# Strassen sums of the right sides: from sums of rows that are then transposed, to sums of transposed blocks

## The chip, the cores and the metric

The kernel runs on one core of a Trainium2 chip. The metric is the device time of one execution in microseconds (us), and the time of a kernel is the median of several executions. The engines are named as the profile names them: PE (TensorE: matmuls and transposes), DVE (VectorE), ACT (ScalarE), POOL (GpSimd) and SP (SyncE, which issues most DMAs).

## The reference, cut to what matters

The reference is one layer of a causal decoder in float32: 1024 positions, width 1024. Two feed-forward blocks (FFNs) of the same form enclose a mixing stage (sparse attention and stick-breaking attention, side by side):

```python
x = x + 0.5 * swiglu(rms_norm(x, g_ffn1), w1_gate, w1_up, w1_down)
...
x = x + 0.5 * swiglu(rms_norm(x, g_ffn2), w2_gate, w2_up, w2_down)

def swiglu(h, w_gate, w_up, w_down):
    return (jax.nn.silu(h @ w_gate) * (h @ w_up)) @ w_down
```

The change touches `h @ w_gate` and `h @ w_up` of both FFNs (w: 1024 x 2816), and of these only how the right sides of the products are made from h.

## The kernel before

**Numbers.** Every matmul of a product is made of three: each operand is split into a high part rounded to the matmul's type (`fp32r`) and a low part, the rest. `halve` makes both: ACT writes the high part into the left half of a tile (L377), DVE or POOL writes source minus high part into its right half (L378). A product is then high x high, high x low and low x high (L468 to L470 in `times`).

**Blocks.** The products are computed transposed, weights on the left and h transposed on the right. h is cut into four blocks of 512 x 512: B11 and B21 are the left and right column halves of the first 512 rows, turned, B12 and B22 those of the last 512. The class `Right` holds them as four tiles of 128 x 1024 (high and low) per block. For the first pair of weight column blocks (p = 0) the products are plain, eight half products, in `opening`; from p = 1 on they follow Strassen's scheme in `products`, with seven products per weight matrix, whose right sides are B11, B21, B22 and the sums T1 = B12 - B11, T2 = B22 - T1, T3 = B22 - B12 and T4 = B21 - T2. So the opening has a second task: to have T1 to T4 ready for the loop.

**How the sums are made before the change.** `Right.sum` subtracts rows that aren't turned (four DVE instructions of 128 x 512 per sum, L435), and `Right.turn` turns the result: 16 transposes on PE (128 x 128 each, L427) into four PSUM banks (`pst`), from which `halve` makes high and low part.

**PSUM.** There are eight banks, two for each letter a, b, c, d. A bank that is asked for again under a letter waits until all that read the one before the last are done. B12 and B22 are turned with letters c and d, T1 to T3 with a and b, c and d being in use for products.

**What sets the order.** In `ffn_in`, the first iteration stands in a manual schedule: PE, DVE, ACT and POOL take their instructions in the order written in `opening`. The loop behind it is ordered by the framework's scheduler. Each engine works its queue in order, and waits at an instruction whose inputs or buffers aren't ready. Transfers are issued by SP, with the loads of weights held back by free buffers and, in the first FFN, the splitting of `w_in` beside the loop paced by matmuls (`beside`).

**Around it.** In the first FFN B11 and B21 are turned at the start, from rows normed right before; in the second, between the two halves of the output projection of the mixing stage (`between`). In both, B12 and B22 are turned in the middle of the opening, once the last rows are normed (L414).

**Names.** In the trace `aB`, `aT`, `ay` belong to the first FFN, `bB`, `bT`, `by` to the second: blocks, sums, rows of B11 and B21. `a00A`, `a10A` are the opening's left sides of gate and up weights, `a01A` and `a01S` those of the loop's first products, `a01s` the sums for them (L457 to L460), `asg` the activated gate and its product with the other side (L522, L525), `as` the sums of the results for the next stage (L589 to L592), `a0u` the accumulated products (L481 to L491).

## Time and profile before

| | us |
|---|---|
| median of three runs | 2219.55 |
| lowest and highest of them | 2217.72, 2219.59 |
| the profiled execution, its own time | 2216.6 |
| its span, first to last instruction | 2214.8 |

| engine | busy us | share of the span | instructions |
|---|---|---|---|
| PE | 2156.8 | 97% | 10460 |
| DVE | 1524.3 | 69% | 2548 |
| ACT | 1103.8 | 50% | 2169 |
| POOL | 858.1 | 39% | 698 |

The first FFN's opening lies from 21 to 82 us, its loop to about 457; the second's opening from about 1562 to 1622. Matmuls are pipelined: a row gives each its own length (0.39 us) although one starts every 0.23, so what a group of them costs is read from starts. A row of the timeline gives start, length, engine, line, what is written and read, count, and in brackets how long the engine had been idle and what released it.

### The profile page before, as it was taken

How to read it: one execution, taken by the hardware profiler on the slowest of the kernel's cores; microseconds unless marked ns; L12 is line 12 of the kernel's file. 1: busy time of each engine (PE TensorE's matmuls, PEld its weight loads, DVE VectorE, ACT ScalarE, POOL GpSimd, SP SyncE). 2: the span in 40 equal slices, each digit the busy share in tenths (PEclk: the TensorE clock that was granted, in tenths of full speed). 3: DMA queues.
4: the chain of work that ended last, by engine and by line, in shares of the span. 5: the costliest groups of instructions: out<-in, count | busy, mean ns of one | idle time of the engine just before them, and what ended most of it. 6: DMA issues, size and time to landing. Idle time of an engine off the chain costs nothing.

```text
span 2214.8 us, 30577 instructions
## 1 busy us (share of the span) xinstructions
PE 2156.8 (97%) x10460; PEld 1800.9 (81%) x10460; DVE 1524.3 (69%) x2548; ACT 1103.8 (50%) x2169; POOL 858.1 (39%) x698
## 2 busy tenths in 40 slices
PE   7999999999999999899999899999999999999999
PEld 6888888888879888688788688878888888888877
DVE  5575767688874598677787687754565555678685
ACT  5333333335454358999987565533333232233443
POOL 3355555523245445211111322264255554552233
PEclk9999999999999999999999999999999999999999
DMA  5487878497675343665654522565133232359655
GB/s 172 94 252 204 243 215 232 169 318 248 213 196 165 112 143 110 202 178 156 168 166 161 199 91 94 204 226 198 63 99 106 94 109 95 113 171 326 225 167 186
DMA packets 269052, 381.01 MB, mean 172 GB/s; under 512 B 23264, under 2 KB 157040, under 8 KB 268896
## 3 DMA queue, kind: packets, MB, share of 16 engines
q1 hardware_dynamic: 256384, 339.17, 49.7%
q0 software_dynamic: 12512, 39.89, 4.9%
q8 instruction: 82, 1.34, 0.3%
q14 instruction: 74, 0.61, 0.1%
HBM read 259.94 MB, written 119.05 MB: 171 GB/s over the span
## 4 chain that ended last, share of the span: by engine, by line
PE 80%; ACT 7%; DVE 6%; DMA 3%; issue 2%; POOL 1%; SPq 0%; ACTq 0%; DVEq 0%; POOLq 0%
PE p L681 6%; PE p L682 6%; PE p L680 5%; PE pc L468 4%; PE pd L468 4%; PE pd L469 4%; PE pd L470 4%; PE pc L469 4%; PE pc L470 4%; PE pa L468 3%; PE pa L469 3%; PE pa L470 3%; ACT junka L1194 3%; PE psf L308 2%; PE psf L309 2%
## 5 line engine op out<-in xcount | busy, mean ns | idle before, releaser
L1194 ACT ACTIVATE junka<-u,cand,sig 128x768 bf16<-128x768 f32 (+4 forms) x186 | 183.7, 988 | 5.6 <-DVE cand L1191 4.0
L1635 DVE TENSOR_TENSOR_SCAN left<-left 128x640 f32<-128x640 f32 (+3 forms) x64 | 86.3, 1349 | 4.0 <-ACT left L1627 4.0
L802 ACT ACTIVATE swh<-swr 128x512 fp32r<-128x512 f32 x48 | 30.2, 628 | 117.2 <-issue 47.8
L1128 POOL DMA_DIRECT2D gd<-evg x32 | 17.9, 561 | 152.6 <-ACT evg L1125 112.8
L803 DVE TENSOR_TENSOR swr<-swr,swh 128x512 f32<-128x512 f32 x48 | 41.1, 856 | 43.0 <-ACT swh L802 42.9
L1684 DVE TENSOR_TENSOR pt<-pstT,pt 128x512 fp32r<-128x512 f32 (+1 forms) x96 | 50.8, 550 | 28.6 <-ACT pt L1682 28.3
L584 ACT ACTIVATE b0u<-b0u 128x512 f32<-128x512 f32 x20 | 12.7, 633 | 95.2 <-DVE b0u L491 78.9
L1684 DVE TENSOR_TENSOR pt<-pspT,pt 128x512 fp32r<-128x512 f32 x72 | 46.8, 684 | 16.3 <-ACT pt L1682 16.3
L1682 ACT ACTIVATE pt<-pspT 128x512 fp32r<-128x512 f32 x72 | 39.7, 596 | 29.2 <-PE pspT L1894 29.2
L681 PE MATMUL p<-bT,bS 128*128 128x512 f32 x132 | 51.5, 390 | 2.8 <-DVE bT L378 2.8
L1815 ACT ACTIVATE e<-e,nm 128x256 f32<-128x256 f32 (+7 forms) x64 | 49.3, 773 | 9.6 <-DVE nm L1810 9.4
L1548 DVE SCALAR_TENSOR_TENSOR u<-relu,WI,u 128x512 f32<-128x512 f32 (+1 forms) x70 | 50.1, 734 | 5.0 <-ACT relu L1541 4.4
L1803 DVE CUSTOM_DVE_ANT_0 e<-psL,bias 128x512 f32<-128x512 f32 (+3 forms) x96 | 49.7, 550 | 5.3 <-PE psL L1840 5.3
L682 PE MATMUL p<-bT,bS 128*128 128x512 f32 x132 | 51.1, 390 | 1.0 <-POOL bS L378 1.0
L681 PE MATMUL p<-aT,aS 128*128 128x512 f32 x132 | 51.4, 389 | 0.0
L1638 DVE TENSOR_TENSOR sa<-sa,left 128x639 f32<-128x639 f32 (+3 forms) x64 | 48.1, 753 | 3.7 <-ACT sa L1629 0.2
L682 PE MATMUL p<-aT,aS 128*128 128x512 f32 x132 | 50.4, 389 | 0.0
L1541 ACT ACTIVATE relu<-psdot 128x512 f32<-128x512 f32 (+1 forms) x80 | 40.1, 520 | 17.9 <-DVE u L1548 8.6
L1682 ACT ACTIVATE pt<-pstT 128x512 fp32r<-128x512 f32 (+1 forms) x96 | 47.0, 518 | 3.3 <-PE pstT L1738 3.1
L1894 PE MATMUL pspT<-ident,e 128*128 128x128 f32 x288 | 39.6, 277 | 8.3 <-DVE ri L1817 5.5
L1629 ACT ACTIVATE sa<-psz 128x512 f32<-128x512 f32 (+2 forms) x96 | 47.0, 511 | 0.1
L1627 ACT ACTIVATE left<-psz 128x512 f32<-128x512 f32 (+2 forms) x96 | 46.2, 506 | 1.6 <-PE psz L1662 1.4
(3021 smaller groups left out, 8228.9 us busy)
## 6 DMA issues: line engine op xcount, KB each, us to landing
aw<-in_w_down_dram SPq DMA_DIRECT2D x33, 512.0 KB, 5.2
bw<-in_w_down_dram SPq DMA_DIRECT2D x33, 512.0 KB, 4.9
swr<-in_w_in_dram SPq DMA_DIRECT2D x48, 256.0 KB, 6.0
a0r<-in_w_gate_dram SPq DMA_DIRECT2D x22, 512.0 KB, 7.1
a1r<-in_w_up_dram SPq DMA_DIRECT2D x22, 512.0 KB, 7.7
b0r<-in_w_gate_dram SPq DMA_DIRECT2D x22, 512.0 KB, 4.2
b1r<-in_w_up_dram SPq DMA_DIRECT2D x22, 512.0 KB, 3.9
x<-in_x_dram SPq DMA_DIRECT2D x16, 512.0 KB, 6.3
```

Of the source, the lines that this page charges most:

```text
L468: nc.tensor.matmul(ps, a[:, c], b[k][:, HI], start=start and k == 0, stop=False, skip_group_check=True)
L469: nc.tensor.matmul(ps, a[:, c], b[k][:, LO], start=False, stop=False, skip_group_check=True)
L470: ins = nc.tensor.matmul(ps, a[:, l], b[k][:, HI], start=False, stop=k == 3, skip_group_check=True)
L680: nc.tensor.matmul(ps[q][m], S[:, h], T[:, HI], start=p == 0, stop=False)
L681: nc.tensor.matmul(ps[q][m], S[:, h], T[:, LO], start=False, stop=False)
L682: nc.tensor.matmul(ps[q][m], S[:, l], T[:, HI], start=False, stop=p == last)
L1194: nc.scalar.activation(junks[1][:, 0:(i + 1) * P], score[i], AF.Sign, scale=sig[:, b:b + 1], bias=cand.bitcast(F32)[:, b:b + 1], accum_out ...
L1548: nc.vector.scalar_tensor_tensor(ac, r, wv, ac, op0=ALU.mult, op1=ALU.add)
L1635: nc.vector.tensor_tensor_scan(back, back, back, 1.0, op0=ALU.mult, op1=ALU.bypass)
L1682: nc.scalar.activation(pt[:, off:512], tp[:, off:512], AF.Copy)
L1684: nc.vector.tensor_sub(pt[:, 512 + off:1024], tp[:, off:512], f32(pt[:, off:512]))
L1803: nc.vector.tensor_tensor_reduce(e[:, c], lp[:, 0:n_], bias[:, c], 1.0, LOW, op0=ALU.add, op1=ALU.max, accum_out=m)
```

## The change

T1 to T4 are no longer turned. Turned copies of B11 and B21 are kept, as they come out of PE, not rounded (`keep`, into the tiles `raw`). T1 is B12's turned block, still in its banks, minus the copy of B11; T2 is B22's, still in its banks, minus T1; T3 is T2 minus the copy of B11, T4 the copy of B21 minus T2, both in SBUF (`less`). `low` makes high and low parts of the sums from SBUF. The values are the same but for the rounding of the differences (T3 is taken as T2 - B11, which is B22 - B12). The copies are made by DVE in the first FFN, by ACT in the second. The pools are cut anew, so that the copies lie where the first rows of x were.

```diff
@@ -384,11 +384,11 @@
 
 
 
-        ROWS = {"B11": (0, 0), "B21": (0, 1), "B12": (1, 0), "B22": (1, 1), "T1": (0, 0), "T2": (0, 0), "T3": (0, 0),
-                "T4": (0, 1)}
-
-        def __init__(self, g, bank, gains, ct, tt, nm):
-            self.g, self.bank, self.gains, self.ct, self.tt, self.nm = g, bank, gains, ct, tt, nm
+        ROWS = {"B11": (0, 0), "B21": (0, 1), "B12": (1, 0), "B22": (1, 1)}
+
+        def __init__(self, g, bank, gains, yt, ct, tt, ts, spare, nm):
+            self.g, self.bank, self.gains, self.yt, self.ct = g, bank, gains, yt, ct
+            self.tt, self.ts, self.spare, self.nm = tt, ts, spare, nm
             self.B, self.y, self.gB = {}, {}, None
 
         def gain(self):
@@ -400,7 +400,7 @@
             self.x, self.half, self.junk, self.rs = xs, half, junk, {}
             for q in range(2):
                 self.y[half, q] = ([xt[:, q * 512:q * 512 + 512] for xt in xs] if half else
-                                   [self.ct(f"{self.nm}y{q}{t}") for t in range(4)])
+                                   [self.yt(f"{self.nm}y{q}{t}") for t in range(4)])
 
         def stat(self, t):
             ss = sm("ss")
@@ -413,26 +413,54 @@
             for c, out_ in ((slice(0, 1024), xt),) if self.half else ((HI, self.y[0, 0][t]), (LO, self.y[0, 1][t])):
                 nc.vector.scalar_tensor_tensor(out_, xt[:, c], self.rs[t], self.gB[:, c], op0=ALU.mult, op1=ALU.mult)
 
-        def operand(self, n):
-            self.B[n] = [self.tt(f"{self.nm}{n}{k}") for k in range(4)]
+        def operands(self, *ns):
+            for n in ns:
+                self.B[n] = [(self.ts if n == "T4" else self.tt)(f"{self.nm}{n}{k}") for k in range(4)]
 
         def turn(self, n, letters="abcd"):
 
-            rows = self.y[self.ROWS[n]]
             if n not in self.B:
-                self.operand(n)
+                self.operands(n)
+            rows, out = self.y[self.ROWS[n]], []
             for k in range(4):
                 ps = self.bank("pst", letters[k % len(letters)])
                 for j in range(4):
                     nc.tensor.transpose(ps[:, j * P:(j + 1) * P], rows[j][:, k * P:(k + 1) * P], ident)
                 halve(self.B[n][k], ps, nc.vector)
-
-        def sum(self, n):
-
-            b11, b21, b12, b22 = (self.y[h, q] for h in range(2) for q in range(2))
-            out, a, b = {"T1": (b11, b12, b11), "T3": (b11, b22, b12), "T2": (b11, b22, b11), "T4": (b21, b21, b11)}[n]
-            for j in range(4):
-                nc.vector.tensor_sub(out[j], a[j], b[j])
+                out.append(ps)
+            return out
+
+        def keep(self, copies, eng=None):
+
+            for t, ps in copies:
+                if eng is nc.vector:
+                    nc.vector.tensor_copy(t, ps)
+                else:
+                    nc.scalar.activation(t, ps, AF.Copy)
+
+        def less(self, to, a, b):
+
+            for t, p, q in zip(to, a, b):
+                nc.vector.tensor_sub(t, p, q)
+
+        def kept(self):
+
+            both = [f32(self.ts(f"{self.nm}raw{k}")) for k in range(4)]
+            self.raw = {"T1": [t[:, LO] for t in both], "T3": [t[:, HI] for t in both],
+                        "T4": [self.ct(f"{self.nm}r21{k}") for k in range(4)]}
+
+        def kept2(self):
+
+            self.raw["T2"] = [self.spare(f"{self.nm}r22{k}") for k in range(4)]
+
+        def low(self, n, eng):
+
+            if n not in self.B:
+                self.operands(n)
+            for t, r in zip(self.B[n], self.raw[n]):
+                nc.scalar.activation(t[:, HI], r, AF.Copy)
+            for t, r in zip(self.B[n], self.raw[n]):
+                eng.tensor_tensor(t[:, LO], r, f32(t[:, HI]), op=ALU.subtract)
 
     def loader(raw, nm):
         def load(w, f, name):
@@ -526,15 +554,20 @@
 
             if "B11" not in B:
                 left(0, "A11")
-                R.operand("B12")
-                R.turn("B11")
+                R.operands("B12", "B11", "B21", "B22", "T1")
+                R.kept()
+                copies = list(zip(R.raw["T3"], R.turn("B11")))
                 left(0, "A12")
-                R.turn("B21")
+                R.keep(copies[0:1], nc.vector)
+                copies += zip(R.raw["T4"], R.turn("B21"))
                 left(0, "A21", "A22")
                 R.second()
             else:
+                copies = []
+                R.operands("B22", "T1")
                 left(0, "A11", "A12", "A21", "A22")
             for t, n in enumerate(("A11", "A12", "A21", "A22")):
+                R.keep(copies[1 + 2 * t:3 + 2 * t], nc.vector)
                 if 4 - t <= len(rows):
                     R.stat(rows[t + len(rows) - 4])
                 left(1, n)
@@ -547,33 +580,35 @@
             half(0, 1, 0, 1)
             gate(1, 0)
             half(1, 0, 0, 0)
-            R.turn("B12", "cd")
+            p12 = R.turn("B12", "cd")
             half(1, 0, 0, 1)
-            R.sum("T1")
+            r = R.raw
+            R.less(r["T1"], p12, r["T3"])
             gated(0, 0)
-            R.turn("B22", "cd")
+            p22 = R.turn("B22", "cd")
+            R.kept2()
             half(1, 1, 0, 0)
+            R.less(r["T2"], p22, r["T1"])
             half(1, 1, 0, 1)
             gated(1, 0)
+            R.low("T1", nc.vector)
+            R.less(r["T3"], r["T2"], r["T3"])
             half(0, 0, 1, 0)
-            R.turn("T1", "ab")
             half(0, 0, 1, 1)
             gate(0, 1)
-            R.sum("T2")
+            R.less(r["T4"], r["T4"], r["T2"])
+            R.low("T2", nc.vector)
             half(0, 1, 1, 0)
-            R.turn("T2", "ab")
             half(0, 1, 1, 1)
             gate(1, 1)
-            R.sum("T4")
-            R.sum("T3")
             half(1, 0, 1, 0)
             half(1, 0, 1, 1)
-            R.turn("T3", "ab")
             gated(0, 1)
             nxt = nxt()
             half(1, 1, 1, 0)
             half(1, 1, 1, 1)
-            R.turn("T4", "ab")
+            R.low("T3", nc.vector)
+            R.low("T4", nc.vector)
             gated(1, 1)
             return [sg[0, 0], sg[0, 1], sg[1, 0], sg[1, 1]], [ct(f"{nm}s{n}") for n in range(3)], nxt
 
@@ -764,13 +799,13 @@
-            tt = of(tpool, "t", 28, dt=F32R)
+            tt, ts = of(tpool, "t", 24, dt=F32R), of(tpool, "ts", 4, dt=F32R)
...
-            R = Right(g_ffn1, bank, fp(op), fp(in_turn((c5, 5), (c3, 3))), tt, "a")
+            R = Right(g_ffn1, bank, fp(op), fp(in_turn((c5, 5), (c3, 3))), ct, tt, ts, early, "a")
...
-                xs.append(fp(tt)(f"x{t}"))
+                xs.append(fp(tt if t > 3 else ts)(f"x{t}"))
...
@@ -2107,12 +2142,13 @@
-            R = Right(g_ffn2, bank, fp(op), ct, tt, "b")
+            R = Right(g_ffn2, bank, fp(op), ct, ct, tt, ts, ct, "b")
 
             def between():
-                R.operand("B12")
-                R.turn("B11")
-                R.turn("B21")
+                R.operands("B12")
+                R.kept()
+                R.keep(zip(R.raw["T3"], R.turn("B11")))
+                R.keep(zip(R.raw["T4"], R.turn("B21")))
```

What the change does to the queues is shown at three places of the first FFN; the second has the same rows with `b` for `a`. In the changed file L553 is the gate product (L525 before), L444 the subtraction in `less`, L461 and L463 the high and the low part in `low`, L485 to L488 the left sides' sums, L496 to L498 the three matmuls, L512, L516 and L519 the additions of products, L624 to L627 the sums of results.

DVE between B12's and B22's turned blocks, before (`aB12`, `aB22`: low parts; `ay0`: rows of T1; the `pst` are the banks):

```order
L378 TENSOR_TENSOR aB123_265<-pst_471,aB123_265 128x512
L435 TENSOR_TENSOR ay00_217<-x4_203,ay00_217 128x512
...
L435 TENSOR_TENSOR ay03_220<-x7_209,ay03_220 128x512
L525 TENSOR_TENSOR asg_408<-asg_408,pa_437 128x512
L378 TENSOR_TENSOR aB220_495<-pst_499,aB220_495 128x512
```

and with the change (`araw`: the copies of B11, and over them T1):

```order
L378 TENSOR_TENSOR aB123_265<-pst_495,aB123_265 128x512
L444 TENSOR_TENSOR araw0_282<-pst_474,araw0_282 128x512
...
L444 TENSOR_TENSOR araw3_285<-pst_495,araw3_285 128x512
L553 TENSOR_TENSOR asg_432<-asg_432,pa_461 128x512
L378 TENSOR_TENSOR aB220_274<-pst_519,aB220_274 128x512
```

The sums stand at the same place of the queue, but read the banks, which are therefore held until the sum is done.

PE from the opening's last matmul (`pd`) into the loop's first products, before:

```order
L470 MATMUL pd_774<-aB223_498,a10A22_376 128x512
L427 MATMUL pst_803<-ident_71,ay10_221 128x128
...
L427 MATMUL pst_824<-ident_71,ay13_224 128x128
L468 MATMUL pc_880<-aT30_708,a01S3_747 128x512
L469 MATMUL pc_880<-aT30_708,a01S3_747 128x512
L468 MATMUL pd_897<-aT10_566,a01S1_748 128x512
```

and with the change:

```order
L498 MATMUL pd_722<-aB223_277,a10A22_400 128x512
L496 MATMUL pa_787<-aB110_266,a01A11_693 128x512
...
L498 MATMUL pb_804<-aT23_627,a01S2_694 128x512
L496 MATMUL pd_837<-aT10_278,a01S1_696 128x512
L497 MATMUL pd_837<-aT10_278,a01S1_696 128x512
L496 MATMUL pc_820<-aT30_747,a01S3_695 128x512
```

The 16 transposes of T4 are gone, as are those of T1, T2 and T3 further up, 64 in each FFN; and the loop's first four products come in another order, those of B11 (`pa`) and T2 (`pb`) ahead of those of T1 (`pd`) and T3 (`pc`).

DVE at the same time, before (`aT4`: low parts of T4):

```order
L525 TENSOR_TENSOR asg_610<-asg_610,pc_683 128x512
L457 TENSOR_TENSOR a01s1_752<-a0r1_743 128x512
...
L460 TENSOR_TENSOR a01s4_755<-a0r1_741,a01s2_753 128x512
L378 TENSOR_TENSOR aT40_799<-pst_803,aT40_799 128x512
...
L525 TENSOR_TENSOR asg_673<-asg_673,pd_774 128x512
L589 TENSOR_TENSOR as0_832<-asg_610,asg_673 128x512
...
L488 TENSOR_TENSOR a0u3_895<-a0u2_862,pc_880 128x512
```

and with the change (`aT3`, `aT4`: low parts; `ar21`: the copies of B21, and over them T4):

```order
L553 TENSOR_TENSOR asg_618<-asg_618,pc_663 128x512
L485 TENSOR_TENSOR a01s1_700<-a0r1_691 128x512
...
L488 TENSOR_TENSOR a01s4_703<-a0r1_689,a01s2_701 128x512
L463 TENSOR_TENSOR aT30_747<-araw0_282,aT30_747 128x512
...
L463 TENSOR_TENSOR aT40_759<-ar210_286,aT40_759 128x512
...
L553 TENSOR_TENSOR asg_661<-asg_661,pd_722 128x512
L624 TENSOR_TENSOR as0_772<-asg_618,asg_661 128x512
...
L516 TENSOR_TENSOR a0u3_835<-a0u2_802,pc_820 128x512
```

T3's low parts have moved behind the left sides' sums, next to T4's, and both now read SBUF alone.

More of the change, by code (lines that the diff above doesn't have):

```diff
@@ L2046, in trunk @@
             tpool = ctx2.enter_context(tc.tile_pool(name="t2", bufs=1, side="right"))
-            tt = of(tpool, "t", 28, dt=F32R)
+            tt, ts = of(tpool, "t", 24, dt=F32R), of(tpool, "ts", 4, dt=F32R)
             fp = lambda place: lambda name: f32(place(name))
@@ L2052, in residual @@
                 for q in range(4):
-                    xs.append(fp(tt)(f"x2{half}{q}"))
+                    xs.append(fp(tt if half else ts)(f"x2{half}{q}"))
                     t = 4 * half + q
```

## The prediction

> **What bounds the kernel now.** The first view read is the table of stretches; its columns are the stretch, its length, then for each engine busy microseconds and instructions, the clock granted to TensorE, the DMA share and GB/s. The first row is the loop of the first FFN with the start of its down projection, the other two are the openings of both FFNs, from the first product with B12's turned blocks to the first product of the loop.
>
> ```profile
> 82.00:520.00 438.00, 438.00 (x1934) 362.59 (x1933) 308.96 (x388) 164.81 (x297) 221.52 (x146) 1.00 0.77 232
> 47.00:88.00 41.00, 41.00 (x215) 34.86 (x214) 26.75 (x40) 14.29 (x27) 10.79 (x8) 1.00 0.19 60
> 1587.00:1628.00 41.00, 41.00 (x215) 34.90 (x214) 26.84 (x40) 14.29 (x27) 10.78 (x8) 1.00 0.18 59
> ```
>
> In both openings PE is busy for 41.00 of 41.00 us at clock 1.00, while DVE works 26.8 us, ACT 14.3 and POOL 10.8; the loop behind is filled by PE as well. So an instruction taken from PE here should shorten the run, and work put on the others is free as long as PE does not come to wait. The second view, the chain of waits, agrees: it goes through the turns that the change removes.
>
> ```profile
> 50.35 1.75 PE pst L427 x16
> ...
> 74.73 1.75 PE pst L427 x16
> ```
>
> These are the turns of T1 and of T4; T2's and T3's stand between them, four pieces of 16 transposes with 1.75 us each.
>
> **What the change removes.** The third view, PE's timeline (start, length, engine, line, tile), prices a turn by what comes after it.
>
> ```profile
> 47.46 0.39 PE L468 MATMUL pc<-aB,a00A 128*128 128x512 f32 x1
> ...
> 49.96 0.40 PE L470 MATMUL pc<-aB,a00A 128*128 128x512 f32 x1
> 50.19 1.91 PE L427 MATMUL pst<-ident,ay 128*128 128x128 f32 x16
> 51.86 0.48 PE L468 MATMUL pc<-aB,a00A 128*128 128x512 f32 x1
> ...
> 81.80 0.39 PE L468 MATMUL pa<-aB,a01A 128*128 128x512 f32 x1
> ...
> 87.24 0.39 PE L468 MATMUL pa<-aB,a11A 128*128 128x512 f32 x1
> ...
> 1587.39 0.39 PE L468 MATMUL pc<-bB,b00A 128*128 128x512 f32 x1
> ...
> 1627.13 0.39 PE L468 MATMUL pa<-bB,b11A 128*128 128x512 f32 x1
> ```
>
> From 81.80 to 87.24 PE issues 24 matmuls with nothing between them: 5.44 / 24 = 0.2267 us each, whatever length a row shows, since they overlap. From 49.96 to 51.86 are 1.90 us where one step would do, so 16 transposes cost 1.67, and the steps just behind them a little. Over the whole opening: from 47.46 to 87.24 are 39.78 us for 96 matmuls of the eight half products and 48 of the first four products; 144 x 0.2267 = 32.64, so 7.14 us are the four turns with what follows them. The second FFN: 1627.13 - 1587.39 = 39.74, less 32.64 = 7.10. **First term: -14.24 us.**
>
> [...]
>
> **What it adds on PE.** T1 and T2 are now taken straight from the banks that hold B12's and B22's turned blocks. B12 and B22 both use banks c, d, c, d; so a bank of B12 comes free for B22 not after its low part (L378) but after the sum that follows on DVE. DVE's timeline, and PE's:
>
> ```profile
> 37.00 2.48 DVE L378 TENSOR_TENSOR aB<-pst,aB 128x512 fp32r<-128x512 f32 x4 [1.05 <-ACT aB L377]
> 39.40 2.49 DVE L435 TENSOR_TENSOR ay<-x,ay 128x512 f32<-128x512 f32 x4
> 40.25 1.91 PE L427 MATMUL pst<-ident,x 128*128 128x128 f32 x16
> ```
>
> The new sums stand where L435 stood and should cost the same 0.60 apart, 0.68 long: done at 40.08, 40.68, 41.28, 41.89. B22's four groups of four transposes would start at 40.25, 40.67, 41.08 and 41.50 (1.67 / 4 = 0.42 apart). With 0.07 for a signal they now start at 40.25, 40.75, 41.35 and 41.96: the last is 0.46 late. Queued behind it on PE is half a product with B12, so all later matmuls shift; who waits for those is the loop. Bounds: 0.2 (no signal time, a sum counted done at its 0.60) and 0.8 (two tenths for each signal). I take 0.46 in both FFNs. **Second term: +0.9 us.**
>
> **What it adds on DVE and ACT, and what covers it.** In the first FFN eight copies of B11's and B21's turned blocks go to DVE, in front of the norms on which B12's turn depends.
>
> ```profile
> 21.26 0.48 PE L468 MATMUL pa<-aB,a00A 128*128 128x512 f32 x1
> 21.45 1.41 DVE L378 TENSOR_TENSOR aB<-pst,aB 128x512 fp32r<-128x512 f32 x2 [0.16 <-ACT aB L377]
> 28.93 0.15 DVE L284 TENSOR_SCALAR ms<-ss 128x1 f32<-128x1 f32 x1 [1.41 <-ACT aj L408]
> 29.01 6.94 DVE L414 SCALAR_TENSOR_TENSOR x<-x,rs,ag 128x1024 f32<-128x1024 f32 x4
> 36.00 1.64 PE L427 MATMUL pst<-ident,x 128*128 128x128 f32 x13 [0.55 <-DVE x L414]
> L414 DVE SCALAR_TENSOR_TENSOR ay<-x,rs,ag x8: 739/745/1740, 7.7 to 15.0; 128x512 f32<-128x512 f32 x8
> L414 DVE SCALAR_TENSOR_TENSOR x<-x,rs,ag x4: 1272/1795/2312, 29.0 to 33.6; 128x1024 f32<-128x1024 f32 x4
> ```
>
> The last two rows are from the view of line L414 (shortest, median and longest, in ns).
>
> No copy from a bank by DVE is in the trace. The nearest row is L378 from a bank, 0.60 apart. One copy between the low parts moves B21's low parts by at most 0.6, and PE reads them only from 21.26 + 12 x 0.2267 = 23.98 on. Seven copies take 4.2 us of the 6.07 between 22.86 and 28.93, where DVE has only three scalar instructions. The last statistic comes from ACT at 28.93 all the same, so nothing moves: I take 0. Low end 0; high end with 1.74 each, the longest row of L414 on 512 elements: seven copies end at 36.2 with the one ahead, the norms start 7.2 late, and PE, which already waits 0.55 there, waits some 7 more, once.
>
> In the second FFN the eight copies go to ACT.
>
> ```profile
> 1537.42 4.03 ACT L377 ACTIVATE bB<-pst 128x512 fp32r<-128x512 f32 x8 [5.00 <-PE pst L427]
> 1540.20 0.48 PE L308 MATMUL psout<-wout110h,m 128*128 128x512 f32 x1
> 1546.72 1.06 ACT L408 ACTIVATE bj<-x 128x1024 bf16<-128x1024 f32 x1 [5.27 <-DVE x L2071]
> ```
>
> Sixteen at 4.03 / 8 = 0.50 end at 1545.5, before ACT's next work at 1546.72. PE needs B11's first bank back at 1540.20; its copy is the fifth in ACT's queue and ends at about 1540.0; the next bank is needed 24 matmuls of 0.2267 later. Cost 0, at most 0.5.
>
> **The late queue on DVE.** T3's and T4's low parts now both stand behind the left sides' sums and ahead of the products' additions. They have two inputs in SBUF, where they had one in a bank. What that does shows in two neighbouring rows of DVE and POOL:
>
> ```profile
> 77.65 2.48 DVE L378 TENSOR_TENSOR aT<-pst,aT 128x512 fp32r<-128x512 f32 x4 [3.24 <-ACT aT L377]
> 78.02 2.55 POOL L378 TENSOR_TENSOR a01A<-a0r,a01A 128x512 fp32r<-128x512 f32 x2
> 80.76 1.60 DVE L589 TENSOR_TENSOR as<-asg 128x512 f32<-128x512 f32 x1
> 81.77 1.74 POOL L378 TENSOR_TENSOR a01S<-a01s,a01S 128x512 fp32r<-128x512 f32 x1
> 82.40 1.66 DVE L590 TENSOR_TENSOR as<-as,asg 128x512 f32<-128x512 f32 x1
> ```
>
> Low parts read from a bank run at full speed beside POOL (2.48 for four, 2.55 for two); sums of two SBUF tiles take 1.60 and 1.66 while POOL works, where four such took 2.49 together at 39.40 without it, and POOL's own 1.27 becomes 1.74. They take turns. [...]
>
> So I lay the opening out anew. Three more rows serve: DVE's gate product ahead of the left sides' sums, and what ACT makes of these.
>
> ```profile
> 71.01 0.68 DVE L525 TENSOR_TENSOR asg<-asg,pc 128x512 f32<-128x512 f32 x1
> 73.30 1.76 ACT L377 ACTIVATE a01S<-a01s 128x512 fp32r<-128x512 f32 x3 [2.74 <-DVE a01s L458]
> 74.96 1.14 ACT L377 ACTIVATE a01A<-a0r 128x512 fp32r<-128x512 f32 x2
> ```
>
> PE starts the half products at 47.46 + 0.46 = 47.92, ends 96 of them at 69.68, has pa and pb at 75.12, reads T3's first low part at 76.25 and the others 0.68 apart to 78.3. It starts product 4, which adds T4 into pc, at 85.55. DVE's gate product follows 60 half-product matmuls and may run at 64.4; ACT's high part of S2 starts at 66.7 (2.3 behind the gate product, as 73.30 to 71.01) and T3's high parts seven activations later, each 0.52 behind the one ahead (two take 1.14, one 0.62); they begin at 70.4. From 71.0 on four of POOL's low parts are left. Taking turns, 0.6 and 1.2 us, T3's low parts end at 71.7, 73.5, 75.3 and 77.1, all 1.2 us or more ahead of PE; T4's end at 80.7. (ACT's copy of pa, at 80.8, takes over a buffer of T4's; PE's second product into pa wants it at 82.8.) Behind them stand the gate product, three sums, two additions and then the one that frees pc, 0.6 to 0.7 each: done at 85.0, and PE wants pc at 85.55. **Cost 0, with 0.55 us to spare;** one contended instruction more (0.95) would make it +0.4 per FFN, five +4.2.
>
> **Sum.** The profiled execution took 2216.6 us, 1.8 more than its span of 2214.8; -14.24 + 0.9 = -13.3 makes it 2203.3. The median of the runs shown, 2219.55, stands 2.95 above that execution; on it the forecast is **2206.2**. The two openings give about equal shares, 6.7 and 6.6.
>
> **The rivals.** *First, PE waits for the late queue* (the taking of turns above, decisive). For it: 0.55 us is thin, and all eight low parts changed side. Against: POOL has four instructions left then. If T3 and T4 cost four contended instructions more, 3.8 us, PE loses 3.8 - 0.55 = 3.2 in each FFN: gain 6.8, time 2212.7; with two, 2208.9. *Second, the copies at the head* cost their high end of 7 us once: 2213.2. Against it: they read a bank, and such rows are not slowed in this trace. *Third, the loop of the first FFN does not follow*, its DMA share of 0.77 being the bound, and 6.7 us are given back: 2212.9. Against it: PE filled 438.00 of 438.00. *Fourth, slower:* the same queue, but with all eight low parts and three finishing sums at 2.31 us, the longest row of L414 above. That is 11 x (2.31 - 0.60) = 18.8 in place of the 4.9 counted, 13.9 more; less 0.55 PE stands 13.3 in each opening and loses 6.7 net: 2219.55 + 13.3 = 2232.9. It decides from a pc freed 7.2 us later than 85.0; below that it only eats the gain. Against: DVE waits only while POOL has something to do, and rows with 512 elements reach 1.66 and 1.74 here. That the change does not do what it says is not open: the order shows 128 transposes fewer.
>
> **How the numbers follow.** Forecast 0.73 (its own range 2203 to 2209: terms -14.24 with 0.4 to 1.6 back, small waits, and the 2.95 between execution and median), first rival 0.13, second 0.04, third 0.04, slower or level by the fourth 0.06. A measurement of this kernel tells about 0.2%, 4.4 us, from no change. Forecast, first, second and third all gain more than that nearly always: faster 0.91; the fourth splits with the edges: same 0.05, slower 0.04. The range, 2202 to 2212, holds the forecast and the milder half of the first rival.
>
> **What would show it.** In the profile after: 16 rows of four turns gone from PE, 47 to 88 still full; the first product of the loop at about 69.7 in place of 76.2; B22's turn stretched from 1.91 to about 2.4 us, released by the DVE sums; copies at about 0.6 each, and the norms still from 29.0; T3's and T4's low parts at about 1.7 beside POOL and 0.6 alone. A wait of PE at product 4 for the addition that frees pc means the first rival; norms that start after 30 the second. The forecast is wrong if PE's idle time in the two openings exceeds 9 us together, or if the first FFN's loop does not end 6 to 7 us sooner.

## The result and the profile after

| | before | after |
|---|---|---|
| median, six executions of each (us) | 2218.95 | 2203.75 |
| lowest and highest | 2216.47, 2220.78 | 2201.85, 2207.88 |
| profiled execution, its span | 2216.6, 2214.8 | 2206.97, 2205.2 |
| PE: busy us, instructions | 2156.8, 10460 | 2146.3, 10332 |
| DVE: busy us, instructions | 1524.3, 2548 | 1536.5, 2556 |

The ratio is 0.9935 with a 95% interval of 0.9925 to 0.9945: faster by 14.4 us (12.2 to 16.6), where 13.3 were forecast; 2206.2 was the predicted time. The changed kernel was timed again with the experiments below, against 15 executions of the kernel before: 0.9942 (0.9929 to 0.9954), which is 12.9 us.

The stretches that the prediction began with, in the changed kernel (length, then busy time and instructions of PE, weight load, DVE, ACT and POOL, the granted clock, the DMA share and GB/s):

```profile
82.00:520.00 438.00, 437.35 (x1930) 361.82 (x1929) 312.96 (x392) 166.81 (x300) 218.87 (x146) 1.00 0.75 235
47.00:88.00 41.00, 41.00 (x183) 33.94 (x182) 30.50 (x43) 13.90 (x25) 12.17 (x8) 1.00 0.29 69
1583.00:1624.00 41.00, 41.00 (x183) 33.96 (x182) 30.58 (x43) 14.22 (x26) 12.42 (x9) 1.00 0.20 65
```

The openings are still full of PE work at clock 1.00: the turns went, and the next products moved up. DVE works some 4 us more in each of these stretches of 41 us, which now reach over 6 us further into the loop's work. PE's timeline at the places the prediction named:

```profile
21.51 0.48 PE L496 MATMUL pa<-aB,a00A 128*128 128x512 f32 x1
36.27 1.64 PE L428 MATMUL pst<-ident,x 128*128 128x128 f32 x13 [0.54 <-DVE x L414]
40.49 2.42 PE L428 MATMUL pst<-ident,x 128*128 128x128 f32 x16
69.99 0.39 PE L496 MATMUL pa<-aB,a01A 128*128 128x512 f32 x1
80.87 0.39 PE L496 MATMUL pa<-aB,a11A 128*128 128x512 f32 x1
85.86 0.39 PE L496 MATMUL pc<-aT,a01A 128*128 128x512 f32 x1
450.79 0.39 PE L715 MATMUL p<-aT,aS 128*128 128x512 f32 x1
...
1532.71 3.65 PE L428 MATMUL pst<-ident,by 128*128 128x128 f32 x32
1576.08 2.42 PE L428 MATMUL pst<-ident,x 128*128 128x128 f32 x16
1986.36 0.39 PE L715 MATMUL p<-bT,bS 128*128 128x512 f32 x1
```

B22's turns are the rows of 2.42 us (1.91 before). The first product of the loop starts at 69.99, the first one with `a11A` at 80.87, and product 4 (into `pc`, 85.86) starts without a wait. Two distances serve as a ruler for every kernel from here on: from the first half product to the start of the first down projection (450.79 - 21.51 = 429.28), and from B11's turn in the second FFN to the start of the second down projection (1986.36 - 1532.71 = 453.65). Each holds one opening and one loop. In the trace of before the same rows stand at

```profile
457.16 0.39 PE L680 MATMUL p<-aT,aS 128*128 128x512 f32 x1
...
1536.79 3.44 PE L427 MATMUL pst<-ident,by 128*128 128x128 f32 x30
1997.05 0.39 PE L680 MATMUL p<-bT,bS 128*128 128x512 f32 x1
```

which with 21.26 makes 435.90 and 460.26: the change gains 6.62 and 6.61, 13.23 us together, against 13.3 in the prediction's sum. The span fell by 9.6 only. Between the two rulers the profiled execution of after took 2.29 us more than that of before (1532.71 - 450.79 against 1536.79 - 457.16), behind the second one 1.09 more (2205.2 - 1986.36 against 2214.8 - 1997.05), and it began the half products 0.25 later. Whether the change costs that is the first question below.

### The profile page after: what moved, and what is told of

Read it like the earlier page. It is cut to its first block, busy times and chain, and to the rows that moved or that the text cites. A ratio compares the mean times of both kernels' runs of the same rounds, so it can differ in the third digit from the quotient of the medians.

```text
span 2205.2 us, 30354 instructions
## 1 busy us (share of the span) xinstructions
PE 2146.3 (97%) x10332; PEld 1789.8 (81%) x10332; DVE 1536.5 (70%) x2556; ACT 1108.7 (50%) x2177; POOL 856.9 (39%) x698
## 4 chain that ended last, share of the span: by engine, by line
PE 57%; DVE 8%; ACT 8%; DMA 3%; issue 3%; POOL 1%; SPq 0%; DVEq 0%; ACTq 0%; POOLq 0%
PE p L716 4%; PE p L717 4%; PE p L715 4%; ACT junka L1229 4%; PE psf L308 2%; PE psf L310 2%; PE psf L309 2%; PE pa L497 2%; PE pc L497 2%; PE pd L497 2%; PE pa L496 2%; PE pc L496 2%; PE pd L496 2%; PE pa L498 2%; PE pd L498 2%
## 5 line engine op out<-in xcount | busy, mean ns | idle before, releaser
L1929 PEld LDWEIGHTS pspT<-ident,e 128*128 128x128 f32 x288 | 34.5, 142 | 15.5 <-issue 5.9
```

The costliest lines, as they stand in the source:

```text
L1929: nc.tensor.transpose(tp[:, q * P:(q + 1) * P], E[n + q][:, j * P:(j + 1) * P], ident)
```

## The experiments

The rulers in all profiles, in us, with the time that each kernel takes from the mixing stage's first product (`pscq`) to its output projection (`psout`):

| kernel | first ruler | second ruler | mixing | ratio to before (95%) |
|---|---|---|---|---|
| before | 435.90 | 460.26 | 794.2 | |
| after | 429.28 | 453.65 | 796.4 | 0.9935 (0.9925 to 0.9945) |
| after, again | 429.37 | 453.66 | 796.7 | 0.9942 (0.9929 to 0.9954) |
| turns put back | 436.50 | 460.78 | 796.1 | 1.0010 (1.0001 to 1.0019) |
| first FFN alone | 429.31 | 460.30 | 794.2 | 0.9968 (0.9955 to 0.9980) |
| ACT copies B12, turns later | 428.98 | 454.15 | 795.6 | 0.9943 (0.9930 to 0.9957) |
| ACT copies B12 | 428.84 | 453.16 | 794.2 | 0.9931 (0.9919 to 0.9943) |
| the same, turns later, gate behind | 428.39 | 453.53 | 794.6 | 0.9934 (0.9922 to 0.9946) |
| T3's and T4's low parts twice | 436.12 | 460.88 | 794.7 | 1.0000 (0.9991 to 1.0009) |
| T4's low parts twice | 433.02 | 455.70 | 795.6 | 0.9964 (0.9950 to 0.9978) |
| copies twice, first FFN | 433.70 | 453.66 | 797.0 | 0.9968 (0.9956 to 0.9979) |

A ruler repeats within 0.1 us from one execution to the next; a whole execution varies by some 6.

### The changed kernel again

> The changed kernel once more, unchanged, for a second profile. Theory (the gain is the turns' time in the two openings, 6.6 and 7.1 us, and what differs elsewhere between the two profiled executions is scatter): ratio to the kernel before 0.9925 to 0.9945; in the trace the stretch from the first half product to the first product of the loop again about 59.4 us in the first FFN (65.98 before), B22's turn 2.42, no wait of PE at product 4; the losses of 1 us in each down projection and of 2 us ahead of the second FFN that the first profile showed come out different. Rival (the change itself costs 1 to 4 us behind the openings, by a later start of other work): the same losses at the same places again.

The rulers came out as 429.37 and 453.66, B22's turn again as 2.42, and product 4 without a wait. Of the losses that the expectation names, the first down projection has none: from its start to the mixing stage are 215.8 us in the first profile and 215.1 in the second, 216.0 before. The other two came back: behind the second ruler are 219.69 us (218.84 in the first profile, 217.75 before), and the mixing stage took 796.7. Taken alone this would speak for the rival. The half products began at 20.39 here, and between 20.4 and 21.6 in all eleven profiles, so the 0.25 at the start is scatter.

Where the 2 us of the mixing stage arise can be read from the traces, for all engines have the same instructions in the same order there. In the first profile PE stays within 0.3 us of the kernel before up to 574 us behind the stage's first product. Then come these rows, of before and then of after; both windows begin 570 us behind that product, and the clock is the third number from the end:

```profile
1244.97 1.23 DVE L1245 TENSOR_TENSOR_SCAN cum<-eq 128x512 f16<-128x512 f16 x1
1243.10:1253.10 10.00, 7.17 (x39) 5.56 (x39) 9.62 (x44) 5.79 (x20) 1.53 (x3) 0.99 0.57 203
```

```profile
1239.55 1.23 DVE L1280 TENSOR_TENSOR_SCAN cum<-eq 128x512 f16<-128x512 f16 x1 [1.34 <-DMA bd<-cum]
1236.60:1246.60 10.00, 5.95 (x27) 4.87 (x27) 8.38 (x39) 4.69 (x17) 1.47 (x3) 0.84 0.48 178
```

DVE stands 1.34 us for a transfer that it did not wait for before, PE behind it 3.52 in place of 2.29, and then a stretch at half the granted clock follows (0.50 from 1243.48 to 1246.90) that the profile of before does not have (1.00 from 1243.20 to 1253.20). Four other profiles have more of the slow clock than before around this place as well: from 1200 to 1245 us the mean granted clock is 0.92 in the changed kernel's second profile and with the turns put back, 0.89 with the change in the first FFN alone and with ACT's copies and the turns later, against 0.96 before. And the first FFN alone, at 794.2, lacks another slow stretch, 31 us into the stage (1.00 from 660 to 705), that before has (0.50 from 703.90 to 707.31). So the stage's time depends on such stretches, and with one profile of before it can't be told whether the one at this place has to do with the change. The times of all kernels can tell whether anything is lost outside the rulers: for each of the ten rows below "before" in the table, the change in time (ratio less one, times the median of before in that round) differs from the change in the two rulers by -1.2 to +1.7 us, and by 0.1 on average. A loss of 2 to 4 us in every execution would show there. The profiled execution of before, at 2216.6, was one of the faster ones (medians of that kernel are 2216.9 to 2219.0). Why DVE's transfer landed later stays open.

### The turns put back, unread

```diff
+        def idle_turn(self):
+            for k in range(4):
+                ps = self.bank("pst", "ab"[k % 2])
+                for j in range(4):
+                    nc.tensor.transpose(ps[:, j * P:(j + 1) * P], ident, ident)
...
             half(0, 0, 1, 0)
+            R.idle_turn()
...
             half(0, 1, 1, 0)
+            R.idle_turn()
...
             half(1, 0, 1, 1)
+            R.idle_turn()
...
             half(1, 1, 1, 1)
+            R.idle_turn()
```

> The changed kernel with four turns of 16 transposes put back in each opening where T1 to T4 were turned before, of a constant tile, and never read: added work, the outputs do not depend on it. Theory (the gain is PE's time for the turns and nothing else): +14.24 us on the changed kernel, so 0.9 us above the kernel before, ratio to it 1.0004, within 0.999 to 1.002. Rival (part of the gain comes from elsewhere, such as DVE's sums of rows or the high and low parts read from banks): the time stays 3 to 10 us below the kernel before, ratio 0.9955 to 0.9985.

The rulers are 7.2 and 7.1 us longer than in the changed kernel, 14.3 together, where the first term of the prediction has 14.24. Against the kernel before they are longer by 0.60 and 0.52: that is the wait for the banks at B22's turn, laid bare, for which the second term has 0.46. (A wait for the late queue, had the changed kernel one, would be hidden again by the turns put back, and the rulers would have grown by less.) The ratio, 1.0010, holds the expected 1.0004 inside its interval. So the gain is PE's time for 64 transposes in each opening, and the work that went to DVE and ACT costs nothing else.

### The change in the first FFN alone

The second FFN has the class and the opening of before, with its pool of 28 tiles; the diff is the change itself, left out there.

> The change in the first FFN alone; the second FFN's opening as it was before. Theory (two independent openings, 6.6 us from the first and 7.1 less 0.46 from the second, both on PE's path): gain 6.6 us, ratio 0.9970 (0.9960 to 0.9980). Rival one (the first FFN's loop, at a DMA share of 0.77, gives it back, and all the gain is the second's): ratio 1.000. Rival two (the gain is the first's alone): ratio 0.9935.

429.31 and 460.30: the first ruler is that of after, the second that of before, to 0.05 us. The ratio is 0.9968, 7.1 us (4.4 to 10.0). The openings add up, and the first FFN's loop follows in full though its DMA share is 0.75 to 0.77. Both rivals are refuted; rival one here is the third rival of the prediction.

### ACT's copies free the banks, and the turns stand later

```diff
             half(1, 0, 0, 0)
-            p12 = R.turn("B12", "cd")
             half(1, 0, 0, 1)
+            p12 = R.turn("B12", "cd")
             r = R.raw
-            R.less(r["T1"], p12, r["T3"])
+            R.keep(zip(r["T1"], p12))
+            R.less(r["T1"], r["T1"], r["T3"])
             gated(0, 0)
+            half(1, 1, 0, 0)
             p22 = R.turn("B22", "cd")
             R.kept2()
-            half(1, 1, 0, 0)
             R.less(r["T2"], p22, r["T1"])
```

> The changed kernel with two edits in both openings: ACT copies B12's turned blocks into T1's tiles and the sum for T1 is taken there, so that B22's banks come free by ACT's copies and not by DVE's sums; and the turns of B12 and B22 each stand one half product later. Theory: B22's turn back from 2.42 to 1.9 to 2.0 us in both FFNs (0.46 each), PE's wait of 0.54 for the norms at B12's turn in the first FFN gone: 1.4 us less than the changed kernel, 2202.3 on its median, ratio 0.9929 to the kernel before; by time alone that can hardly be told from the changed kernel, the trace decides. Rival (the banks are late for the next reader in place of that: the first product with B12 wants a bank of B22's one half product after its turn, and T2's sum has to be through): PE waits at that product, 0.5 to 2 us in each FFN, and the time is that of the changed kernel or above.

PE's timeline of this kernel, the turns of B12 and B22, and the first product with B12:

```profile
36.90 1.91 PE L428 MATMUL pst<-ident,x 128*128 128x128 f32 x16
41.41 1.91 PE L428 MATMUL pst<-ident,x 128*128 128x128 f32 x16
...
45.69 0.39 PE L498 MATMUL pb<-aB,a10A 128*128 128x512 f32 x1
46.80 0.47 PE L496 MATMUL pc<-aB,a00A 128*128 128x512 f32 x1 [0.72 <-DVE ar L444]
```

Both happened. The turns take 1.91 without a wait ahead of them, and the next to use a bank, the first product with B12, stands still in their place, released by T2's sum: 0.72 us by its row, and 0.88 by starts (45.69 to 46.80 where 0.23 would do). In the first FFN 0.3 us remain of the gain (428.98), in the second it is a loss of 0.5 (454.15), for there B12's turn had no wait to lose.

### ACT's copies alone

```diff
-            R.less(r["T1"], p12, r["T3"])
+            R.keep(zip(r["T1"], p12))
+            R.less(r["T1"], r["T1"], r["T3"])
```

> The changed kernel with one edit in both openings: ACT copies B12's turned blocks out of the banks, and T1's sum is taken from the copies; the turns stay where they are. Theory (B22's turn waits for the DVE sum and nothing else; ACT is idle there from 38.7 to 41.1): B22's turn back from 2.42 to 1.91 us, 0.5 in each opening, the next readers not late: the stretch from B22's turn to the first product with B12 0.5 us shorter in both; 1.0 us below the changed kernel, ratio 0.9935 to the kernel before, not to be told by time. Rival (the banks of B12 or B22 are late for someone else): the 0.5 comes back as a wait at the first product with B12, as it did with the turns one half product later.

```profile
39.51 1.91 PE L428 MATMUL pst<-ident,x 128*128 128x128 f32 x16
...
1571.64 1.91 PE L428 MATMUL pst<-ident,x 128*128 128x128 f32 x16
```

B22's turn takes 1.91 in both FFNs, and the rulers are shorter by 0.5 each (428.84 and 453.16). The second term is thereby shown by its removal: it was the DVE sum that held the banks, 1.0 us in all. Median 2202.39, ratio 0.9931: level with the changed kernel within the intervals. It is the better kernel by its rulers, not by a measured time.

### ACT's copies, the turns later, and the gate product behind

The edit, against the kernel with ACT's copies and the turns later:

```diff
             R.less(r["T1"], r["T1"], r["T3"])
-            gated(0, 0)
...
             R.less(r["T2"], p22, r["T1"])
+            gated(0, 0)
```

> The kernel with ACT's copies and both turns one half product later, and besides the first gate product on DVE behind T2's sum in place of ahead of B22's low parts. Theory (in that kernel the 0.72 us that PE waits at the first product with B12 is the gate product of 0.60 in the queue ahead): the wait falls to about 0.12 us in both openings, 1.2 us below that kernel and 1.3 to 1.4 below the changed kernel, 2202.4, ratio to the kernel before 0.993; by time hardly to be told from the changed kernel. Rival (the sum is held by something else, the low parts waiting for ACT's high parts): the wait stays 0.5 us or more.

```profile
46.78 0.39 PE L498 MATMUL pb<-aB,a10A 128*128 128x512 f32 x1
47.29 0.47 PE L496 MATMUL pc<-aB,a00A 128*128 128x512 f32 x1
```

The row at 46.78 ends at 47.17, so the wait before 47.29 is 0.12 where it was 0.72, as the theory has it; the rival is refuted. By starts 0.51 are left of 1.11, and the 0.60 between them is the gate product. Against the kernel with the turns later the rulers are 0.59 and 0.62 us shorter, 1.2 together as expected. Against the changed kernel 0.9 us are gained in the first FFN and 0.1 in the second, 1.0 where 1.3 to 1.4 were expected.

### T3's and T4's low parts twice

```diff
-                eng.tensor_tensor(t[:, LO], r, f32(t[:, HI]), op=ALU.subtract)
+                for _ in range(2 if n in ("T3", "T4") else 1):
+                    eng.tensor_tensor(t[:, LO], r, f32(t[:, HI]), op=ALU.subtract)
```

> The changed kernel with each of the eight low parts of T3 and T4 subtracted twice (the same values; added work on DVE's late queue only). Theory (the late queue has 0.6 us to spare against product 4, POOL is through with its share by then, so that the extra ones cost 0.6 each): 8 x 0.6 = 4.8 us more on DVE, PE waits 4.8 - 0.6 = 4.2 us in each opening, in part already at T3's product and the rest at product 4: 8.4 us above the changed kernel, 2212, ratio to the kernel before 0.9970 (0.996 to 0.998). Rival one (the queue has much more room than the prediction laid out): no change against the changed kernel, ratio 0.994. Rival two (the extra ones take turns with POOL too, 1.74 each): 13.9 - 0.6 = 13.3 us in each opening, 2230, ratio 1.006.

The late queue is the point where PE comes to wait, as the theory has it, and the price was too low: the rulers grew by 6.8 and 7.2 us, 14.0 in all, and the ratio is 1.0000. DVE first, of the changed kernel and then of this one:

```profile
71.25 6.05 DVE L463 TENSOR_TENSOR aT<-araw,aT 128x512 fp32r<-128x512 f32 x4 [3.28 <-ACT aT L461]
77.23 3.59 DVE L463 TENSOR_TENSOR aT<-ar,aT 128x512 fp32r<-128x512 f32 x4
84.58 0.68 DVE L516 TENSOR_TENSOR a0u<-a0u,pc 128x512 f32<-128x512 f32 x1
```

```profile
70.53 9.79 DVE L464 TENSOR_TENSOR aT<-araw,aT 128x512 fp32r<-128x512 f32 x8 [3.28 <-ACT aT L461]
80.23 5.40 DVE L464 TENSOR_TENSOR aT<-ar,aT 128x512 fp32r<-128x512 f32 x8
86.88 0.69 DVE L839 TENSOR_TENSOR swr<-swr,swh 128x512 f32<-128x512 f32 x1
89.88 0.68 DVE L517 TENSOR_TENSOR a0u<-a0u,pc 128x512 f32<-128x512 f32 x1
```

Eight more cost 3.74 + 1.81 = 5.55 in place of 4.8, the extra ones of T3 meeting POOL, and in the first FFN a subtraction for the splitting of `w_in` (L839) slips in ahead. PE's timeline, and the granted clock behind the waits:

```profile
85.05 0.50 PE L497 MATMUL pa<-aB,a01A 128*128 128x512 f32 x1 [2.02 <-ACT a0u L510]
90.62 0.50 PE L497 MATMUL pc<-aT,a01A 128*128 128x512 f32 x1 [2.54 <-DVE a0u L517]
93.22 0.63 PE L499 MATMUL pc<-aT,a01A 128*128 128x512 f32 x1
...
1629.16 0.79 PE L497 MATMUL pc<-bT,b01A 128*128 128x512 f32 x1 [4.39 <-DVE b0u L517]
```

```profile
90.62:91.65 1.03, 1.03 (x4) 0.86 (x5) 1.03 (x2) 0.27 (x1) 0.00 (x0) 1.00 0.49 48
91.65:94.93 3.28, 3.28 (x10) 2.53 (x8) 2.13 (x4) 2.59 (x6) 1.52 (x1) 0.52 0.60 126
1629.16:1634.44 5.28, 5.28 (x12) 4.13 (x13) 3.17 (x5) 3.82 (x8) 2.48 (x2) 0.50 0.14 53
```

Neither the theory nor a rival has this size. One wait is ACT's: its copy of `pa` takes over a buffer of T4's, and stands behind the low parts for it; the prediction had this in a parenthesis with 2 us to spare. And behind the waits comes something new: from 91.65 on matmuls start 0.43 apart in place of 0.23, for 3.3 us, at a granted clock of 0.52, and for 5.3 us at 0.50 in the second FFN. That is some 1.6 us more in the first opening (3.28 x 0.48) and 2.6 in the second (5.28 x 0.50); with waits of 4.56 and 4.39 they make 6.1 of the 6.8 and 7.0 of the 7.2. The rest of the first is in the steps at the ends of its two waits.

### T4's low parts twice

The edit is that of the kernel before, for T4 alone.

> The changed kernel with the four low parts of T4 alone subtracted twice (the same values; added work). With T3's and T4's twice, PE waited 2.02 + 2.54 us in one opening and 4.39 in the other, and behind these waits the granted clock was 0.52 and 0.50 for 3 to 5 us. Theory (the queue lacks 4 x 0.6 - 0.6 = 1.8 us in each opening, up to 2.4 in the first where a fifth instruction may slip in ahead; a wait of that length does not yet bring the slow clock, since matmuls ran at full clock behind the 2.02): PE waits 1.8 to 2.4 in each opening and the clock stays 1.00; the stretch from the first half product to the down projection is 1.8 to 2.4 us longer than in the changed kernel in both FFNs, 4 us in all, ratio to the kernel before 0.9955. Rival (any wait of about 2 us brings the slow clock): another 1.5 to 2.7 us in each opening, 8 us in all, ratio 0.9975.

```profile
87.65 0.51 PE L497 MATMUL pc<-aT,a01A 128*128 128x512 f32 x1 [1.76 <-DVE a0u L517]
...
1627.09 0.50 PE L497 MATMUL pc<-bT,b01A 128*128 128x512 f32 x1 [1.74 <-DVE b0u L517]
```

```profile
87.65:88.65 1.00, 1.00 (x4) 0.85 (x5) 1.00 (x2) 0.00 (x0) 0.00 (x0) 1.00 0.38 65
88.65:91.95 3.30, 3.30 (x9) 2.59 (x9) 2.64 (x5) 2.37 (x5) 1.03 (x1) 0.52 0.49 86
...
1627.09:1630.40 3.31, 3.31 (x14) 2.74 (x15) 3.22 (x6) 1.78 (x4) 0.43 (x1) 1.00 0.24 84
1630.40:1633.70 3.30, 3.30 (x16) 2.73 (x15) 1.25 (x2) 3.30 (x8) 3.30 (x3) 1.00 0.00 0
```

The wait is as expected, 1.76 and 1.74: four low parts, less the spare 0.6. Neither expectation holds for the clock: behind the one wait it drops to 0.52 for 3.3 us, behind the other, of nearly the same length and at the same instruction, it stays at 1.00. The rulers say the same, 3.7 us longer in the first FFN and 2.0 in the second.

### The copies at the head twice

```diff
-                    nc.vector.tensor_copy(t, ps)
+                    for _ in range(2):
+                        nc.vector.tensor_copy(t, ps)
```

> The changed kernel with the eight copies of B11's and B21's turned blocks in the first FFN made twice on DVE (the same values; added work). Theory (the copies are covered by DVE's idle time ahead of the last statistic, of which the profile of the changed kernel leaves 0.19 + 0.21 + 0.21 + 0.21 + 0.81 = 1.6 us): 4.8 us more, 3.2 of it uncovered, the norms start at about 32.4 in place of 29.3 and PE waits 3.7 us in place of 0.54 at B12's turn; 3.2 us above the changed kernel, once, ratio to the kernel before 0.9955. Rival (the place of the norms is not on PE's path, and other work fills PE): no wait added.

The last statistic and the norms behind it on DVE, of the changed kernel and then of this one:

```profile
29.19 0.15 DVE L284 TENSOR_SCALAR ms<-ss 128x1 f32<-128x1 f32 x1 [0.81 <-ACT aj L408]
29.27 6.95 DVE L414 SCALAR_TENSOR_TENSOR x<-x,rs,ag 128x1024 f32<-128x1024 f32 x4
```

```profile
32.74 0.15 DVE L284 TENSOR_SCALAR ms<-ss 128x1 f32<-128x1 f32 x1
32.80 6.33 DVE L414 SCALAR_TENSOR_TENSOR x<-x,rs,ag 128x1024 f32<-128x1024 f32 x4
```

The norms start at 32.80, where 32.4 was expected. This kernel began its half products 0.38 us earlier (21.13 against 21.51), so they come 3.9 us later behind these and not 3.2: the copies stand 0.66 us apart here in place of 0.60. In the changed kernel the last statistic still comes from ACT, 0.81 after DVE was free for it; here DVE is late by itself. PE's timeline of this kernel at B12's turn:

```profile
35.79 0.33 PE L428 MATMUL pst<-ident,x 128*128 128x128 f32 x1 [0.70 <-DVE x L414]
37.99 0.33 PE L428 MATMUL pst<-ident,x 128*128 128x128 f32 x1 [1.88 <-DVE x L414]
39.18 2.99 PE L428 MATMUL pst<-ident,x 128*128 128x128 f32 x13 [0.87 <-DVE x L414]
```

PE waits 3.45 in three pieces, and then 13 transposes take 2.99 where the changed kernel has 1.64. The first ruler is 4.4 us longer in place of 3.2: 2.9 more of waiting, and the rest again behind a slow clock:

```profile
39.00:42.20 3.20, 3.02 (x14) 3.02 (x15) 1.72 (x4) 1.79 (x3) 0.00 (x0) 0.54 0.33 100
```

The cover that the prediction claimed for the copies was there, and about as thick as its rows said.

## Why the prediction was right

The forecast was 13.3 us by its sum; by the rulers of the profiled executions it is 13.23, and by the times 14.4 and 12.9, with intervals that hold it.

- **What bounds the kernel.** PE, in both openings and both loops. From the loop's first product with `a11A` to the down projection are 369.92 us before (87.24 to 457.16); after, 80.87 to 450.79 is 369.92 again. So nothing gained in an opening is given back in its loop.
- **First term, -14.24.** Measured 14.3 by putting the transposes back. The division by starts (0.2267 for a matmul, 7.1 for four turns) held to 0.1 us.
- **Second term, +0.9.** The timeline shows 2.42 - 1.91 = 0.51 at each B22 turn; taking away its cause returns 0.44 to 0.53 and 0.49 to 0.50. 0.46 was a few hundredths low in each FFN. Where it took 0.07 for a signal from DVE to PE, for which it shows no row, the trace has 0.15: T1's sums end at 40.94, 41.53 and 42.13, and the groups of transposes that wait for them start at 41.08, 41.68 and 42.28. At B12's turn in the trace of before it is 0.05 (35.95 to 36.00).
- **Copies at the head, 0.** Right. The copies from banks cost 0.60 apart, one or two standing between statistics. PE's wait at B12's turn is 0.54, as before 0.55. In the second FFN ACT's sixteen end at 1541.3, 1.3 us ahead of its next work:

```profile
1539.08 2.21 ACT L439 ACTIVATE br<-pst 128x512 f32<-128x512 f32 x4
1542.58 1.06 ACT L408 ACTIVATE bj<-x 128x1024 bf16<-128x1024 f32 x1 [1.29 <-DVE x L2106]
```

- **The late queue, 0 with 0.55 to spare.** T3's low parts were laid out to end between 71.7 and 77.1, and the trace has 6.05 us for four from 71.25 on. POOL is beside them until 78.46:

```profile
71.60 3.45 POOL L378 TENSOR_TENSOR a01A<-a0r,a01A 128x512 fp32r<-128x512 f32 x2
...
76.72 1.74 POOL L378 TENSOR_TENSOR a01S<-a01s,a01S 128x512 fp32r<-128x512 f32 x1
```

  The addition that frees `pc` ends at 85.26 and PE takes it at 85.86: 0.60 to spare. That the margin is real, and no wider, is what the doubled low parts show. The taking of turns with POOL, which the prediction read from the 1.60, 1.66 and 1.74 of the trace of before, holds in these rows: beside POOL the low parts from SBUF are 1.78 us long and start 1.70 apart (only the first, 0.95, met the end of a POOL instruction), alone they are 0.60 apart.
- **Two readings that were off, without effect.** DVE's gate product follows 72 half-product matmuls and not 60; the 64.4 that the layout gives it fits 72 (64.75 in the trace). The two rows of 41 us that are called the openings end behind the loop's fourth product and not at its first.
- **What was mis-sized.** Not a term of the sum, but a price in the rivals. The first and the fourth let PE's wait cost its own length; with four low parts more it cost 1.76 and then another 1.9 in the first opening, and the doubled eight cost 14.0 us in place of 8.4 expected. Had the late queue been late by 3.2 us in each opening, as the first rival has it, the gain would have been smaller than its 6.8, by up to some 4 us (an estimate from the 1.6 and 2.6 us that the slow clock cost behind the waits of 4.56 and 4.39). The forecast itself has no such wait and was not touched.
- **The profiled execution.** 2203.3 was forecast for it, and it took 2206.97. The 3.6 between lie outside the openings and their loops (2.29 in the middle, 1.09 at the end, 0.25 at the start). The medians came out nearer to the sum, and on the other side of it: 2.4 us below 2206.2, of which 0.6 is the median of before in that round (2218.95 in place of 2219.55) and the rest lies within the interval. To add a term to one execution's time carries that execution's luck.

## What to carry to other kernels

Price an instruction on a full engine by the distance of starts with it and without it, not by the length in its row: a turn of sixteen transposes, 1.91 us in its row, was worth 1.78 (7.1 for four). When a sum is moved to read the bank itself, the bank's next writer then waits for that sum (B22's turn took 2.42 us in place of 1.91); look for an idle engine that can copy the block out, as ACT could here for half a microsecond in each opening. Measure a change of half a percent in a kernel that scatters by 6 us on distances inside the trace that hold the change and little else; they repeated within 0.1 us, where half a dozen executions leave an interval of 2 us to either side. What such a distance leaves out has to be looked for in the times, and over all kernels timed, not in two profiles.

## What the runs showed of the hardware that was not expected

A wait of PE can cost more than its length. Behind waits of 1.76, of 2.02 and 2.54, and of 4.39 us, and behind three waits of 0.70, 1.88 and 0.87 in a row, the granted clock fell to 0.50 to 0.54 for 3.2 to 5.3 us, with matmuls 0.43 apart in place of 0.23; behind a single wait of 1.74 it did not (1.00 from 1627.09 to 1633.70), behind the 2.02 alone the clock was still 1.00 (85.05 to 86.05), and behind the openings' waits of up to 0.72 no sign of it is seen (1.00 from 21.50 to 88.00 in the changed kernel, with its wait of 0.54; matmuls 0.23 apart behind the 0.72). In two of the cases the slow stretch begins about 1 us after PE has resumed (at 88.7 and at 91.7) and lasts 3.4 us. Behind the 4.39 it began within the wait, at 1627.8, and lasted to 1634.6, 6.8 us, twice as long.

The traces of before and after have slow stretches outside the openings too, five and seven within the span, at a granted clock of 0.50. Each is 3.41 or 6.83 us long, and within each trace all their edges lie whole multiples of 3.413 us apart (in the changed kernel 697.35, 700.76, 751.96, 758.79 and so on: 1, 16 and 18 of them behind the first). In the 3.41 us ahead of each of the twelve PE was busy for 1.49 us or less; from 898.74 to 902.15 in the changed kernel it was busy for 1.55, and behind that the clock stayed at 1.00. Why the wait of 1.76 was followed by the slow clock and the one of 1.74 was not, the runs do not show.
